# Five of six modulation groups summed on VectorE instead of TensorE

## The chip, the cores and the metric

The kernel runs on one core of one Trainium2 chip. The core has five engines with a queue of instructions each: TensorE (matrix products), VectorE, ScalarE, GpSimd and SyncE, which issues most DMAs. The metric is the device time of one execution in microseconds (us), as the median of three runs.

## The reference, cut to what matters

The reference has two blocks, a two-layer latent transformer and a block that ends in a mixture of experts, on 256 tokens of 1024 features. What the change touches is the modulation of the first block: two vectors (one for the latents, one for the context) times a 1024 x 6144 matrix per layer.

```python
silu_c = jax.nn.silu(c)
silu_cc = jax.nn.silu(c_ctx)
for layer in range(DEPTH):
    mod = (silu_c @ w_mod[layer] + b_mod[layer])[:, None, :]
    mod_c = silu_cc @ w_mod[layer] + b_mod[layer]
    shift1, scale1, gate1, shift2, scale2, gate2 = jnp.split(mod, N_MOD, axis=-1)
    c_shift1, c_scale1, c_gate1, c_shift2, c_scale2, c_gate2 = jnp.split(mod_c, N_MOD, axis=-1)
    ...
    h = modulate(rms_norm(x, norm_mix[layer]), shift1, scale1)
    ...
    x = x + gate1 * x_mix
    x = x + gate2 * swiglu(modulate(rms_norm(x, norm_ffn[layer]), shift2, scale2),
                           w_gate_up[layer], w_down[layer])
```

In the last layer the context stream is only used for its keys and values, so only c_shift1 and c_scale1 of that layer are needed.

## The kernel before, in words

Activations lie feature by feature: 128 features on the partitions, tokens along the free axis, eight chunks for the 1024 features. Layer 0 handles latents and context together (512 columns), layer 1 only the latents (256 columns, apart from the keys and values of the context). Every weight unit and every activation is split in two float32r parts, and a product is three matmuls (`mm3`). The first part is written by ScalarE, the second (source minus first part) by VectorE; `divide` does both.

The program is a set of Python generators, and a planner writes out the order of the instructions at build time. Class `Timer` (line 213) estimates when each engine is through; `stall` (511) says how long TensorE would wait for something; `drive` (525) steps the first generator whose inputs are there; `fill` (553) makes a step of a queue of side work when nothing else is ready, and `background` (566) makes one after each weight unit of a `gemm` (623). `tick` (473) emits deferred VectorE work whose inputs are there, and the weight loads and splits. `finish` (587) drives a queue to its end at once. All engine calls go through one wrapper, so that nearly every instruction has line 288; tiles tell them apart.

The modulation of one layer comes in three groups of 16 feature chunks, and each group has 16 tiles of w_mod: [128 rows of chunk k, 1024 columns], 512 KB. `modulation` (798) runs over the eight k and two halves. For each tile it makes two matmuls on quarters of the array: the 32 columns of `cs` (the two activated vectors, the rest zeros) times 512 columns of w_mod, summed in one PSUM tile over k. Then ScalarE copies the sums, TensorE turns them, and VectorE adds the bias into `mod`. In the trace these matmuls read `u,cs`; each float32 matmul has two records, so a chunk has four.

Group 0 of layer 0 runs at the start, where the first norm needs it. The other groups are entries of `self.bg`: groups 1 and 2 of layer 0 from line 1410 on, to be finished before the output projection (1447); group 0 of layer 1 during layer 0's feed-forward part (1472); groups 1 and 2 of layer 1 during layer 1 (1410). So a chunk stands where `background` or `fill` put it, and the rest where `finish` forces it. w_mod is loaded two tiles ahead (1411), ten ahead for one stretch (1451).

All big tiles share a pool of 42 buffers `u` of 4 KB per partition. SyncE issues the loads in order, and a load waits until the earlier users of its buffer are through. The second block ends with the experts, whose weights are streamed through the same buffers (`pump`, 1944).

Of the kernel before, what the change touches and what calls it, by code (L numbers as in the profile page):

```python
# [2 lines left out]

# [7 lines left out]
F32 = mybir.dt.float32  # L11
# [22 lines left out]
# ---------------------------------------------------------------- host layout  # L34
# [6 lines left out]
def _units(w):  # L41
    """[K, N] -> [N/128, 128 rows, K/128, 128 columns]"""
    k, n = w.shape
    return np.ascontiguousarray(w.reshape(k // 128, 128, n // 128, 128).transpose(2, 1, 0, 3))


def column_parameters(p):
    """Every per-feature vector as columns of one [128, n] array, and where each one starts."""
# [32 lines left out]
def shape_tables():  # L81
    t = {}
    # axial rotary embedding of the first block, feature-major; the sign of the pair swap is in the sine
# [8 lines left out]
    # discrete Fourier transform on odd frequencies  # L92
# [7 lines left out]
    # filter positions and decay  # L100
# [10 lines left out]
    # rotary embedding of the second block: inverse frequency and sign of the swapped half, per partition  # L111
# [4 lines left out]
    # 8 * log of how many of the dilated branches let query i see key j  # L116
# [6 lines left out]
    # before[t', t] = t' < t; descending weights that break ties; slot numbers  # L123
# [45 lines left out]
# ---------------------------------------------------------------- order of the program  # L169

class Null:
    """Stands for every object of the program in the pass that only finds the order of the weight tiles."""
# [22 lines left out]
class Part:  # L195
    """The two float32r parts of a tile.  ready: the n pieces of the program that fill it are there; eta: when they
    are expected to have run."""
# [15 lines left out]
class Timer:  # L213
    """Estimates when each engine will be through with its instructions, and when each tile will be there."""
# [48 lines left out]
    def there(self, x):  # L263
        if isinstance(x, float):
            return x
        if isinstance(x, Part):
            if x.ready:
                return self.there(x.ap)
            return FAR if x.eta is None else x.eta
        if not isinstance(x, bass.AP):  # L270
            return 0.0
        return self.wrote.get(x.name, (0.0, ""))[0] + self.LAG


class Engine:
    """An engine whose instructions are also given to the timer."""
# [26 lines left out]
class Stream:  # L303
    """The weight tiles that one chain of generators uses, in their order.  Loads run ahead; a unit (128 columns) is
    split ahead into two float32r parts."""
# [20 lines left out]
    def prepare(self):  # L326
        """split the next unit"""
# [8 lines left out]
    def run(self):  # L336
        """loads and splits ahead"""
# [13 lines left out]
    def get(self, *key, unit=True):  # L351
        """the next tile: a generator, which ends with the tile, or with the two parts of a unit"""
# [23 lines left out]
class Squares:  # L376
    """Sums of the squares of x for each token.  x comes in four pairs of chunks, each [128, 2, T] cut as gemm cuts
    its output; the first three are added up before they are summed over the partitions"""
# [39 lines left out]
class Net:  # L418
    TOL = 0.15
    EASE = 1.5  # L420
    PACE = 1.5
# [10 lines left out]
    def __init__(self, tc, a, at, orders, dbg, stop):  # L432
# [5 lines left out]
        self.fillers, self.bg = [], []  # L438
# [8 lines left out]
    # ---- allocation  # L447
# [16 lines left out]
    def ahead_of(self, n):  # L464
        """split n weight units ahead"""
        self.W.loads, self.W.splits = n + self.MORE, n

    # ---- order of the instructions
    def defer(self, fn, *deps, engine="DVE"):
        """fn emits instructions of an engine once deps are expected to be there when the engine comes to them"""  # L470
        self.pending.append((deps, engine, fn))

    def tick(self):
        """deferred instructions whose inputs are there; loads and splits of weights"""
# [11 lines left out]
        for s in self.streams:  # L486
            s.run()
        while len(self.piece) < self.ahead and t.free["DMA"] < t.free["PE"] + 2:
# [8 lines left out]
    def force(self):  # L497
        """the deferred instructions whose inputs are there first"""
# [12 lines left out]
    def stall(self, deps):  # L511
        """how long the tensor engine would wait"""
# [3 lines left out]
    def step(entry):  # L516
        """one step of [generator, what the step reads]; False if it can do nothing yet, None at its end"""
# [7 lines left out]
    def drive(self, *gens, extra=()):  # L525
        """all of the generators to their ends: the first of those whose inputs are there makes a step.  A generator
        yields what its next step reads, or BLOCK.  extra: entries that come second, but need not end"""
# [25 lines left out]
    def fill(self, *queues):  # L553
        """a step of the first entry of a queue, if its inputs are there"""
# [11 lines left out]
    def background(self):  # L566
        """a step of the work that only has to be done some time later"""
# [3 lines left out]
    def wait(self, *deps):  # L571
        """steps of the fillers while the tensor engine would wait"""
# [5 lines left out]
    def run(self, gen):  # L578
        """a generator to its end, with the fillers in its gaps"""
# [7 lines left out]
    def finish(self, queue):  # L587
        while queue:
            self.tick()
            if self.step(queue[0]) is None:  # L590
                queue.pop(0)

    # ---- pieces
    def divide(self, items, parts=(), then=None):
        """hi = float32r(src), lo = src - hi for each (hi, lo, src) or (hi, lo, src, factor of src); then the
        parts are ready"""
# [26 lines left out]
    def gemm(self, keys, xs, T=512, n=None, cuts=None, together=False, stream=None):  # L623
        """unit . xs for each weight unit, as a list of PSUM tiles [128 features, n units, T]; a generator.  xs may
        still grow to n; with cuts xs is a list of lists, and the k range between two cuts has its own output;
        together: the units side by side, each chunk of xs used as soon as it is there"""
# [50 lines left out]
    def pair(name, *idx, tail=()):  # L677
        """the two units of a pair of chunks: the last index counts pairs"""
# [3 lines left out]
    def by_tile(t, T):  # L682
        """[128, 2 chunks, T] cut as gemm cuts its output"""
# [5 lines left out]
    def pairs(self, T):  # L689
        """an endless row of tiles [128, 2, T]"""  # L690
# [5 lines left out]
    def chunks(self, n, T, pieces=1):  # L696
        """n places for the two float32r parts of [128, T]; and the parts of each two as gemm cuts its output"""
# [18 lines left out]
    def token_sums(self, ps, accs, first=True, last=True):  # L716
        """ps[128 tokens, tile] = sum over the partitions (and over accs) of acc[:, tokens]"""
# [6 lines left out]
    def rsqrt(self, ps, n, mul, add):  # L724
        """(ps*mul + add) ** -0.5"""
# [6 lines left out]
    def spread(self, ps, r):  # L732
        """ps[:, token] = r[token] in every partition"""
# [3 lines left out]
    def rms(self, accs, width, eps=1e-6):  # L737
        """PSUM tile with the reciprocal root mean square of each token in every partition"""
# [5 lines left out]
    def spread_rms(self, ps, width, eps=1e-6):  # L744
        """the same from the sums of the squares"""
# [7 lines left out]
    def modulated(self, xs, rb, gain, shift, out, streams=(0, 1), early=False):  # L753
        """parts of x*rb*gain + shift for pairs x[128, 2, T]; gain, shift: functions (chunk, stream) -> column;
        early: all the x*rb in a first step"""
# [28 lines left out]
    def norm_gain(self, xs, rb, name, out):  # L784
        """parts of x*rb*gain for x in pairs [128, 2, 256]"""
# [11 lines left out]
    # ---- modulation  # L797
    def modulation(self, l, grp):
        """columns grp*16 .. grp*16+15 (of 128 features) of both modulation vectors"""
# [29 lines left out]

    def gain_columns(self, l, which, m):  # L830
        """norm gain * (1 + scale)"""
        g = self.cp.tile([128, KC, 2], F32, name=f"g{which}{l}")
        for s in range(2):
# [4 lines left out]
    # ---- hyena filter and its spectrum  # L838
    def sin_of(self, ps, i):
        """sin(freq*(ps + b)) for [128, 256]"""  # L840
# [8 lines left out]
    def reduce_angle(self, r, a, n):  # L849
        """r = a - 2*pi*round(a / 2*pi), within [-pi, pi]"""  # L850
# [15 lines left out]
    def dft_tables(self, which, use, shape, **axes):  # L866
        """the two parts of a table; a generator"""
# [14 lines left out]
    def spectra(self, z, w1, w23):  # L882
        """spectra of the hyena filters of both layers; the layers' hidden units are in the two halves"""
# [44 lines left out]
    # ---- first block: one layer  # L928
# [1432 lines left out]
```

## Time and profile before

| | |
|---|---|
| median of 3 runs | 2087.15 us (2084.54 to 2092.17) |
| profiled execution, its span | 2082.8 us |
| instructions | 28349 |
| TensorE matmuls busy | 1986.3 us (95%) |
| TensorE weight loads busy | 1450.8 us (70%) |
| VectorE busy | 945.7 us (45%) |
| ScalarE busy | 718.3 us (34%) |
| HBM read | 428.13 MB, 207 GB/s over the span |

The profiled execution is known by its span, from the first to the last instruction; what lies around it is in the times of the runs alone, whose median is 4.35 us longer. A timeline row gives the start, the length, the engine, the line, the operation with the tiles it writes and reads, and how many instructions were merged; in square brackets the idle time before it and what ended it. Busy time of TensorE counts pipelined matmuls whose ends are modelled.

### The profile page before, as it was taken

The numbers are of one execution on the slowest core, as the hardware profiler recorded it, in microseconds if no ns is written. First come the engines' busy times: TensorE is split into PE (matmuls) and PEld (weight loads), VectorE is DVE, ScalarE is ACT, GpSimd is POOL, SyncE is SP. The second block draws the span as 40 slices with busy tenths as digits, with TensorE's granted clock in tenths as the row PEclk, the third lists the DMA queues.
The fourth block names the chain that finished last, engine by engine and source line by source line (L and its number), as shares of the span: only waits on it lengthen the run. The fifth ranks groups of instructions, "written<-read, shape, count | busy, mean of one in ns | idle before, by whom it ended". The sixth has DMA issues, their size and how long they took to land. (4 is left out here: it accounts for less than half of the span.)

```text
span 2082.8 us, 28349 instructions
## 1 busy us (share of the span) xinstructions
PE 1986.3 (95%) x11415; PEld 1450.8 (70%) x11415; DVE 945.7 (45%) x1624; ACT 718.3 (34%) x1171; POOL 39.8 (2%) x49
## 2 busy tenths in 40 slices
PE   7999999999999999999999999999999898888886
PEld 3777877776778888889888999998799541111111
DVE  6665755145334333576764755568654310000001
ACT  3433665224222322363653543444734110000001
POOL 0000000000000000000000000000010000000000
PEclk9999999999999999999999999999999999999999
DMA  9423224464223233444357455553257999999997
GB/s 366 132 81 101 62 82 150 164 236 174 96 88 114 89 91 100 134 170 149 114 188 245 164 189 172 178 183 94 100 167 295 377 419 420 419 419 419 419 420 318
DMA packets 121438, 432.13 MB, mean 207 GB/s; under 512 B 13654, under 2 KB 14152, under 8 KB 121304
## 3 DMA queue, kind: packets, MB, share of 16 engines
q1 hardware_dynamic: 119464, 424.64, 55.7%
q0 software_dynamic: 1696, 5.38, 0.8%
q8 instruction: 91, 1.49, 0.3%
q14 instruction: 43, 0.35, 0.0%
q10 hardware_dynamic: 144, 0.26, 0.0%
HBM read 428.13 MB, written 2.10 MB: 207 GB/s over the span
## 5 line engine op out<-in xcount | busy, mean ns | idle before, releaser
L288 PE MATMUL ps<-u 128*128 128x256 f32 (+2 forms) x9088 | 1599.8, 345 | 28.1 <-DMA u<-w 15.9
L288 PEld LDWEIGHTS ps<-u 128*128 128x128 f32 (+1 forms) x9088 | 1289.0, 186 | 348.1 <-DMA u<-w 101.3
L288 DVE TENSOR_TENSOR u<-u 128x1024 fp32r<-128x1024 f32 (+4 forms) x414 | 433.1, 1071 | 269.6 <-ACT u L288 226.2
L288 ACT ACTIVATE u<-u 128x1024 fp32r<-128x1024 f32 (+3 forms) x392 | 360.3, 960 | 286.9 <-DVE u L288 237.0
L288 PE MATMUL ps<-u,t 128*32 128x512 f32 (+1 forms) x1028 | 214.9, 610 | 30.8 <-DMA u<-w 18.2
L288 PEld LDWEIGHTS ps<-u,t 128*32 128x32 f32 (+1 forms) x1028 | 44.2, 110 | 185.8 <-DMA u<-w 114.5
L288 ACT ACTIVATE u<-ps 128x512 f32<-128x512 f32 (+3 forms) x207 | 91.7, 488 | 237.0 <-PE ps L288 236.3
L288 DVE TENSOR_TENSOR t<-t,ps 128x512 f32<-128x512 f32 x12 | 8.3, 688 | 258.9 <-PE ps L288 258.9
L288 ACT ACTIVATE t<-ps 128x512 f32<-128x512 f32 x57 | 33.4, 595 | 252.5 <-PE ps L288 252.4
L288 DVE TENSOR_TENSOR u<-u,ps 128x512 f32<-128x512 f32 x53 | 36.4, 687 | 128.4 <-PE ps L288 128.3
L288 PE MATMUL ps<-u,cs 128*32 128x512 f32 x384 | 86.1, 644 | 0.0
L288 DVE TENSOR_TENSOR u<-ps,u 128x128 fp32r<-128x128 f32 (+2 forms) x135 | 59.6, 491 | 48.9 <-ACT u L288 42.7
L288 DVE SCALAR_TENSOR_TENSOR u<-ps,mod,u 128x256 f32<-128x256 f32 x96 | 41.7, 479 | 79.9 <-PE ps L288 79.6
L288 ACT ACTIVATE u<-t 128x512 fp32r<-128x512 f32 (+1 forms) x74 | 41.8, 592 | 102.9 <-DVE t L288 91.7
L288 ACT ACTIVATE u<-ps,s 128x512 fp32r<-128x512 f32 (+1 forms) x26 | 15.8, 640 | 149.0 <-PE ps L288 145.8
L288 DVE SCALAR_TENSOR_TENSOR u<-ps,s,u 128x512 fp32r<-128x512 f32 (+2 forms) x24 | 15.4, 662 | 113.2 <-ACT u L288 90.9
L288 ACT ACTIVATE t<-ps,s 128x256 f32<-128x256 f32 (+1 forms) x80 | 49.1, 620 | 41.2 <-DVE s L288 40.2
L288 POOL TENSOR_TENSOR s<-s,mhalf 128x4 f32<-128x4 f32 (+2 forms) x25 | 28.5, 1141 | 1608.4 <-DVE s L288 1527.1
L288 PE MATMUL ps<-ident,t 128*128 128x128 f32 x332 | 46.8, 275 | 9.5 <-DVE t L288 7.0
L288 ACT ACTIVATE t<-u 128x512 f32<-128x512 f32 x41 | 25.2, 627 | 85.3 <-DVE u L288 85.2
L288 PEld LDWEIGHTS ps<-ident,t 128*128 128x128 f32 x332 | 37.8, 141 | 23.6 <-DVE t L288 14.3
L288 DVE TENSOR_REDUCE s<-ps 128x1 f32<-128x512 f32 (+2 forms) x65 | 38.9, 621 | 33.2 <-PE ps L288 32.9
(126 smaller groups left out, 682.6 us busy)
## 6 DMA issues: line engine op xcount, KB each, us to landing
u<-w SPq DMA_DIRECT2D x381, 512.0 KB, 9.9
u<-w_in SPq DMA_DIRECT2D x102, 512.0 KB, 3.9
u<-w_mod SPq DMA_DIRECT2D x96, 512.0 KB, 5.0
u<-w_gu SPq DMA_DIRECT2D x88, 512.0 KB, 3.7
u<-w_dn SPq DMA_DIRECT2D x32, 512.0 KB, 3.5
u<-w_out SPq DMA_DIRECT2D x24, 512.0 KB, 4.5
u<-w_oa SPq DMA_DIRECT2D x16, 512.0 KB, 4.0
u<-w_dn SPq DMA_DIRECT2D x16, 384.0 KB, 3.1
```

The costliest lines, as they stand in the source:

```text
L288: return fn(*args, **kw)
```

## The change

A new generator, `modulation_sums`, takes the place of `modulation` for five of the six groups. For each half of a group it keeps one accumulator [128, 1024] in a `u` buffer for each vector that is needed: both vectors for the groups 1 and 2 of layer 0 and group 0 of layer 1, only the latents' for groups 1 and 2 of layer 1. VectorE multiplies the tile of chunk 0 by the column of `cs` (TENSOR_SCALAR), and adds each further chunk with one SCALAR_TENSOR_TENSOR (tile times column plus accumulator). That makes 16 accumulators, 16 + 112 operations. Then TensorE sums the partitions: 32 columns of ones times 512 columns of an accumulator, two matmuls for each vector on quarters of the array, ten times in all. Copy, four transposes and bias follow as before, for half a group at a time.

The generators sit in a queue of their own, `self.sums`, which `tick` steps whenever the planner believes that TensorE would not wait for the step; each vector operation yields VectorE's estimated end less 0.3 us, and the tolerance is 0.15. w_mod is loaded three tiles ahead throughout. `finish(self.sums)` stands where `finish(self.bg)` does. `rotary_tables` and `memory_norm` stay in `self.bg`. The rest of the diff removes comments.

```diff
+    BEHIND = 0.3
...
     def tick(self):
...
         for s in self.streams:
             s.run()
+        while self.sums and not self.dry and self.stall(self.sums[0][1]) <= self.TOL:
+            if self.step(self.sums[0]) is None:
+                self.sums.pop(0)
...
+    def modulation_sums(self, l, grp):
+        nc = self.nc
+        vectors = (0, 1) if (l, grp) in ((0, 1), (0, 2), (1, 0)) else (0,)
+        for half in range(2):
+            acc = [self.u([128, 1024]) for _ in vectors]
+            for k in range(KC):
+                w = yield from self.W_mod.get("w_mod", l, grp, k, half, unit=False)
+                for s, a in zip(vectors, acc):
+                    c = self.cs[:, k, s:s + 1]
+                    if k == 0:
+                        nc.vector.tensor_scalar(a, w, c, None, op0=OP.mult)
+                    else:
+                        nc.vector.scalar_tensor_tensor(a, w, c, a, op0=OP.mult, op1=OP.add)
+                    yield (lambda: self.timer.free["DVE"] - self.BEHIND,)
+                del w
+            yield acc
+            ps = self.ps()
+            for i, (s, b) in enumerate((s, b) for s in vectors for b in range(2)):
+                nc.tensor.matmul(ps[32 * i:32 * i + 32, :], self.ones32, acc[s][:, b * 512:(b + 1) * 512],
+                                 start=True, stop=True, tile_position=(0, 32 * i))
+            del acc, a
+            n = 64 * len(vectors)
+            t = self.tmp()
+            nc.scalar.activation(t[:n], ps[:n], AF.Copy)
+            yield (t,)
+            pt = self.ps()
+            for b in range(4):
+                nc.tensor.transpose(pt[:, b * n:(b + 1) * n], t[:n, b * 128:(b + 1) * 128], self.ident[:n, :n])
...
+            for s in vectors:
+                nc.vector.tensor_add(m[:, :, :, s], src[:, s, :, :, 0], bias)
+            yield
...
-                self.W_mod.loads = 2
...
-        self.bg = self.before[l, 1]
-        self.W_mod.loads = 2
+        self.bg, self.sums = self.before[l, 1], self.sums_before[l, 1]
+        self.W_mod.loads = 3
...
         self.finish(self.bg)
+        self.finish(self.sums)
...
-        if l == 0:
-            self.W_mod.loads = 10
...
-            self.before = {(0, 1): entry(*m0), (0, 2): entry(m1[0], self.rotary_tables(), self.memory_norm()),
-                           (1, 1): entry(*m1[1:]), (1, 2): []}
+            self.sums_before = {(0, 1): entry(*m0), (0, 2): entry(m1[0]), (1, 1): entry(*m1[1:]), (1, 2): []}
+            self.before = {(0, 1): [], (0, 2): entry(self.rotary_tables(), self.memory_norm()), (1, 1): [], (1, 2): []}
```

How the order moves, at two places. First TensorE, from the end of layer 0's mix to its feed-forward part, before. `u` are weights and activations, `u,cs` the modulation, `ones` and `ident,s` the statistics of the norm between the output projection and the feed-forward part:

```order
L288 MATMUL ps<-u 128x512 x48
L288 MATMUL ps<-u,cs 32x512 x10
L288 MATMUL ps<-ident,t 128x128 x4
L288 MATMUL ps<-u 128x512 x168
L288 MATMUL ps<-ones,acc 128x1 x4
L288 MATMUL ps<-u 128x512 x24
L288 MATMUL ps<-ones,t 128x1 x8
L288 MATMUL ps<-ident,s 128x128 x4
L288 MATMUL ps<-u,cs 32x512 x20
L288 MATMUL ps<-u 128x512 x72
L288 MATMUL ps<-u,cs 32x512 x2
```

The same place now, from the last sum of layer 0's groups, which stands early in the mix, to the first sum of layer 1's group 0:

```order
L289 MATMUL ps<-u,ones_87 32x512 x4
L289 MATMUL ps<-u 128x512 x12
L289 MATMUL ps<-ident,t 128x128 x4
L289 MATMUL ps<-u 128x512 x552
L289 MATMUL ps<-ones_87,acc 128x1 x4
L289 MATMUL ps<-u 128x512 x24
L289 MATMUL ps<-ones_87,t 128x1 x8
L289 MATMUL ps<-ident,s 128x128 x4
L289 MATMUL ps<-u 128x512 x204
L289 MATMUL ps<-u,ones_87 32x512 x4
```

The ten forced matmuls and their transposes before the output projection are gone, and nothing stands between the statistics and the feed-forward part.

Second VectorE, in layer 0's first projections, where the short convolutions read PSUM (`ps,cols`) and weights are split (`u<-u 128x1024`), before:

```order
L288 TENSOR_TENSOR u<-u 128x1024 x3
L288 SCALAR_TENSOR_TENSOR t<-ps,cols,t 128x2x255 x4
L288 TENSOR_TENSOR u<-u,t 128x512 x2
L288 TENSOR_TENSOR u<-u 128x1024 x2
L288 SCALAR_TENSOR_TENSOR u<-ps,cols,u 128x2x255 x4
```

The same place now:

```order
L289 TENSOR_TENSOR u<-u 128x1024 x3
L289 SCALAR_TENSOR_TENSOR u<-u,cs 128x1024 x6
L289 SCALAR_TENSOR_TENSOR t<-ps,cols,t 128x2x255 x4
L289 TENSOR_TENSOR u<-u,t 128x512 x2
L289 TENSOR_TENSOR u<-u 128x1024 x2
L289 SCALAR_TENSOR_TENSOR u<-u,cs 128x1024 x4
L289 SCALAR_TENSOR_TENSOR u<-ps,cols,u 128x2x255 x4
```

Ten new operations (`u<-u,cs`) have come between the old ones, whose order is kept.

## Rows read from the trace of the kernel before

**Rows 1.** Page, part 1: engine, busy us, share of the span, instructions.

```profile
PE 1986.3 (95%) x11415; PEld 1450.8 (70%) x11415; DVE 945.7 (45%) x1624; ACT 718.3 (34%) x1171; POOL 39.8 (2%) x49
```

**Rows 2.** Table of stretches: us, busy time of each engine, clock, DMA share, GB/s.

```profile
51.00:357.00 306.00, 304.28 (x1485) 240.16 (x1484) 189.26 (x402) 151.31 (x286) 8.57 (x6) 0.99 0.30 97
518.00:690.00 172.00, 171.80 (x756) 136.72 (x757) 72.08 (x106) 50.57 (x67) 2.64 (x3) 1.00 0.32 105
882.00:1145.00 263.00, 260.95 (x1912) 227.78 (x1911) 170.62 (x301) 135.17 (x225) 8.29 (x7) 1.00 0.51 173
1640.00:2083.00 443.00, 379.04 (x1720) 96.72 (x1714) 35.80 (x59) 27.14 (x49) 1.29 (x2) 0.99 1.00 407
```

**Rows 3.** TensorE's timeline around one modulation chunk in layer 0's mix.

```profile
393.82 1.05 PE L288 MATMUL ps<-u,cs 128*32 128x512 f32 x4
394.80 11.18 PE L288 MATMUL ps<-u 128*128 128x512 f32 x48
```

**Rows 4.** Page, part 5: the modulation's matmuls; busy us, mean ns, idle before.

```profile
L288 PE MATMUL ps<-u,cs 128*32 128x512 f32 x384 | 86.1, 644 | 0.0
```

**Rows 5.** TensorE's timeline at the end of layer 0's mix.

```profile
454.28 2.77 PE L288 MATMUL ps<-u,cs 128*32 128x512 f32 x20
457.75 0.66 PE L288 MATMUL ps<-ident,t 128*128 128x128 f32 x4 [0.70 <-ACT t L288]
458.16 2.10 PE L288 MATMUL ps<-u 128*128 128x512 f32 x8
```

**Rows 6.** TensorE's timeline at layer 1's start and at its mix's end.

```profile
895.11 2.77 PE L288 MATMUL ps<-u,cs 128*32 128x512 f32 x20
897.81 2.42 PE L288 MATMUL ps<-u 128*128 128x256 f32 x18
...
1145.52 1.06 PE L288 MATMUL ps<-u,cs 128*32 128x512 f32 x8
...
1148.71 3.47 PE L288 MATMUL ps<-u 128*128 128x256 f32 x27
```

**Rows 7.** VectorE's timeline: second parts of the normed input, layers 1 and 0.

```profile
896.55 2.49 DVE L288 TENSOR_TENSOR u<-t,u 128x512 fp32r<-128x512 f32 x4
...
517.46 4.90 DVE L288 TENSOR_TENSOR u<-t,u 128x512 fp32r<-128x512 f32 x8
```

**Rows 8.** TensorE's timeline between layer 0's statistics and its feed-forward part.

```profile
508.93 1.11 PE L288 MATMUL ps<-ident,s 128*128 128x128 f32 x4 [1.38 <-POOL s L288]
509.97 6.79 PE L288 MATMUL ps<-u,cs 128*32 128x512 f32 x40
...
518.20 2.10 PE L288 MATMUL ps<-u 128*128 128x512 f32 x8 [1.00 <-DVE u L288]
```

**Rows 9.** Table of stretches, TensorE alone: us, busy, granted clock, DMA share, GB/s.

```profile
508.00:509.00 1.00, 0.07 (x1) 0.50 1.06 434
...
514.00:515.00 1.00, 1.00 (x12) 0.68 0.76 266
515.00:516.00 1.00, 1.00 (x16) 1.00 1.05 426
```

**Rows 10.** VectorE's instructions by shape: count, busy us, mean ns, idle before.

```profile
L288 DVE TENSOR_TENSOR u<-u 128x1024 fp32r<-128x1024 f32 x301 | 359.4, 1221 | 238.8 <-ACT u L288 197.5 <-issue 23.0 <-PE ps L288 17.5
L288 DVE TENSOR_TENSOR u<-u 128x512 fp32r<-128x512 f32 x71 | 48.2, 689 | 20.3 <-ACT u L288 19.1
...
L288 DVE SCALAR_TENSOR_TENSOR t<-u,cols,t 128x256 f32<-128x256 f32 x60 | 25.0, 478 | 0.0
...
L288 DVE TENSOR_SCALAR t<-t,s 128x512 f32<-128x512 f32 x19 | 9.2, 487 | 0.7
```

**Rows 11.** Waits of TensorE, 51 to 1160 us: total us, times, longest.

```profile
PE ps L288 <- DVE u L288: 4.7, 4, 1.6
```

**Rows 12.** Instructions on w_mod: time from issue to landing of its loads.

```profile
DMA to landing us min/median/max: 3.4/5.0/10.7
```

More of the change, by code (lines that the diff above doesn't have):

```diff
@@ L2 @@
 import itertools
+import types
 import numpy as np
@@ L270, in there @@
         if not isinstance(x, bass.AP):
-            return 0.0
+            return x() if isinstance(x, types.FunctionType) else 0.0
         return self.wrote.get(x.name, (0.0, ""))[0] + self.LAG
@@ L437, in __init__ @@
         self.pending = collections.deque()
-        self.fillers, self.bg = [], []
+        self.fillers, self.bg, self.sums = [], [], []
         self.ahead, self.piece, self.todo = 0, collections.deque(), self.pieces()
@@ L589, in finish @@
             self.tick()
-            if self.step(queue[0]) is None:
+            if queue and self.step(queue[0]) is None:
                 queue.pop(0)
@@ L828, in modulation @@
         yield
+    def modulation_sums(self, l, grp):
[26 more added lines that the diff above has]
+                nc.tensor.transpose(pt[:, b * n:(b + 1) * n], t[:n, b * 128:(b + 1) * 128], self.ident[:n, :n])
+            src = pt[:, :4 * n].rearrange("p (b v i s) -> p v i b s", b=4, v=len(vectors), i=2)
+            m = self.mod[l][:, grp * 16 + half * 8:grp * 16 + half * 8 + 8, :].rearrange("p (i b) s -> p i b s", b=4)
+            bias = self.col(f"b_mod{l}", grp * 16 + half * 8, 8).rearrange("p (i b) -> p i b", b=4)
+            for s in vectors:
+                nc.vector.tensor_add(m[:, :, :, s], src[:, s, :, :, 0], bias)
+            yield
     def gain_columns(self, l, which, m):
         g = self.cp.tile([128, KC, 2], F32, name=f"g{which}{l}")
-        for s in range(2):
+        for s in range(1 if (l, which) == (1, "ffn") else 2):
             self.nc.vector.scalar_tensor_tensor(g[:, :, s], self.mod[l][:, m * 8:m * 8 + 8, s], 1.0,
@@ L1447, in layer @@
         self.finish(self.bg)
+        self.finish(self.sums)
         gate1 = lambda j, s: mod[:, 16 + j, s:s + 1]
         sums = Squares(self, T)
-        if l == 0:
-            self.W_mod.loads = 10
         if l:
@@ L1471, in layer @@
             pass
-        self.bg = self.before[l, 2]
+        self.bg, self.sums = self.before[l, 2], self.sums_before[l, 2]
         self.drive(self.ffn(l, h, T, then))
@@ L2310, in program @@
             self.rope_t = cp.tile([128, 2, SEQ], F32, name="rope_t")
-            self.ones = cp.tile([128, 1], F32, name="ones")
-            nc.vector.memset(self.ones, 1.0)
+            self.ones32 = cp.tile([128, 32], F32, name="ones32")
+            nc.vector.memset(self.ones32, 1.0)
+            self.ones = self.ones32[:, 0:1]
             self.mhalf = cp.tile([128, 8], F32, name="mhalf")
@@ L2323, in program @@
             entry = lambda *gens: [[g, ()] for g in gens]
-            m0, m1 = ([self.modulation(l, g) for g in range(l == 0, 3)] for l in range(2))
+            m0, m1 = ([self.modulation_sums(l, g) for g in range(l == 0, 3)] for l in range(2))
             self.start_second()
-            self.before = {(0, 1): entry(*m0), (0, 2): entry(m1[0], self.rotary_tables(), self.memory_norm()),
-                           (1, 1): entry(*m1[1:]), (1, 2): []}
+            self.sums_before = {(0, 1): entry(*m0), (0, 2): entry(m1[0]), (1, 1): entry(*m1[1:]), (1, 2): []}
+            self.before = {(0, 1): [], (0, 2): entry(self.rotary_tables(), self.memory_norm()), (1, 1): [], (1, 2): []}
             self.layer(0, sums[0], self.squares(sums[1], 512), entry(spectra))
```

## The prediction

> **What bounds the kernel now.** I read the busy times first: TensorE 1986.3 of 2082.8 us, VectorE 945.7 [rows 1]. So TensorE is the suspect, and the next question is whether it is so at the place that changes. The table of stretches answers it [rows 2]: in the stretches of the first block that hold the moved work (51 to 357, 518 to 690, 882 to 1145 us) TensorE is busy 304.3 of 306, 171.8 of 172 and 261.0 of 263 us, and VectorE 189.3, 72.1 and 170.6 us. The last stretch, 1640 to 2083, has another bound: the DMA share is 1.00 at 407 GB/s.
>
> [...] A row on the moved matmuls themselves settles it here: a plain matmul after such a step starts 0.98 us after the step did (393.82 to 394.80), with no idle time named [rows 3]. That is time on the path, and the sum below goes by it.
>
> **What is removed.** All 96 chunks of w_mod cost TensorE 86.1 us, in 384 records, four to a chunk [rows 4]. 16 chunks are group 0 of layer 0, which stays. The other 80 stand in the timeline as 58 steps alone among other matmuls, and four runs of 5, 10, 5 and 2 steps.
> - 58 alone, 0.98 us each [rows 3]: 56.8 us.
> - Run of 5 at the end of layer 0's mix, forced there: 454.28 to 458.16 with the wait for ScalarE and the transposes, 3.9 us [rows 5]. The next matmuls need the last merged chunk, which is made in this time too; I take 3.0.
> - Run of 2 at the end of layer 1's mix: 1145.52 to 1148.71, 3.2 us [rows 6]; I take half, 1.6, for the same reason.
> - Run of 5 at 895.11 to 897.81 [rows 6]: it fills the wait for the normed input, whose second parts VectorE makes from 896.55 on [rows 7]. I take 0.6 of 2.7.
> - Run of 10 at 509.97 [rows 8]: it fills the wait for layer 0's second norm. VectorE makes the second parts from 517.46 on [rows 7], and TensorE waits for them until 518.20 even with the filler. Worth 0.
> - Transposes of the three other groups, 0.4 us each (457.75 to 458.16) [rows 5]: 1.1.
>
> Removed: 56.8 + 3.0 + 1.6 + 0.6 + 1.1 = 63.1 us.
>
> **What is added to TensorE.** Ten sums over the partitions. Six have four matmuls of 32 columns; eight records in a run took 1.06 us [rows 6], taken as 1.0. Four have two, 0.98 us [rows 3]. Together 9.9. Four transposes each, 0.4 us [rows 5], 3.8. Their copies on ScalarE have other matmuls behind them in the new order, so nothing for these; if the cover is gone, each is worth the 0.70 us of the old wait [rows 5].
>
> [...]
>
> **What is added to VectorE.** Sixteen accumulators: 16 TENSOR_SCALAR and 112 SCALAR_TENSOR_TENSOR of 128x1024. No row has this shape. One with two SBUF operands took 478 ns at 256 columns, and a TENSOR_TENSOR goes from 689 ns at 512 to 1221 at 1024, so 1.04 ns a column [rows 10]: 0.478 + 768 x 0.00104 = 1.28 us alone. Bounds are 1.22 (the TENSOR_TENSOR itself) and 1.91 (four times 478). I take 1.22, nearest to the row of the same length, since neighbours overlap a little. TENSOR_SCALAR took 487 ns at 512; between that and twice it, 0.75. Sum: 112 x 1.22 + 16 x 0.75 = 149 us.
>
> It goes 74, 37 and 37 us to the three stretches (64, 32 and 32 operations). The stretches become shorter by what TensorE saves: about 293, 169 and 241 us. VectorE would be busy 263 of 293 (90%), 109 of 169 (64%) and 208 of 241 (86%). It fits, but tightly, and the planner fills whatever gap it believes in, up to 0.45 us beyond TensorE's own time. Queued behind such an operation are second parts of weights (two units ahead, so harmless), second parts of activations, softmax sums, and the four or two matmuls that wait for an accumulator. TensorE now waits for VectorE 4.7 us in four waits over 51 to 1160 us [rows 11]. One operation in front of an urgent one costs up to 1.22 us. Bounds: 0, if every one falls into a real gap, and 137 us, if all 112 come in the way. I take 12 us, ten late ones of 1.22: one for each of the ten sums, where the new order makes TensorE wait for the accumulator itself. That is nearer to zero because the row nearest to it is the 4.7 us.
>
> Loads: the 80 transfers stay, three ahead in place of two (ten at one place). They land in 5.0 us median, 10.7 at most [rows 12], and now VectorE waits for them in order. Priced at nothing while three ahead cover it; else it is part of the first rival.
>
> **Sum.** 63.1 - 9.9 - 3.8 - 2.9 - 12 = 34.5 us. The profiled execution's span is 2082.8 us, so 2048.3; the median of the runs is 4.35 us above that span, so 2087.15 - 34.5 = 2052.7, say 2053. The saving lies before the last stretch, whose DMAs set the end; it carries over because the experts' loads wait for buffers that earlier work frees, and the order of the second block is the same in both programs.
>
> **Rivals.**
> - VectorE gives the saving back. Its place is 51 to 357 us, where it would be 90% busy. The saving without lateness is 46.5 us; at 1.22 us each it is gone when 38 of the 112 operations stand before something urgent, or when loads that land at 10.7 in place of 5.0 us hold VectorE about eight times. For it: the gaps there are small. Against: 64% and 86% elsewhere. Gives 2067 to 2098.
> - The same decides for slower. At 47 operations in the way (57 us) the time is 2098, at 56 (68 us) it is 2109. This needs VectorE to be the bound in attention, where most of its work is softmax that TensorE waits for.
> - Half rate. The scalar-tensor-tensor at half rate takes the time of 1024 more columns, 1.22 + 1.07 = 2.3 us. Then VectorE needs 324 of 293 us in the first stretch: 31 us late there and some 15 more in layer 1, so 34.5 - 46 = -12, 2099. The row of 478 ns at 256 columns against it: half rate would add 256 columns at 1.04 ns and make 0.74. [...]
> - More than forecast: no lateness at all, and the covered runs worth half: 2030 to 2041.
> - The change does not do what it says, since the DMA-bound end begins when it began: 2087. Against it stands that its loads follow the buffers.
>
> **How the numbers follow.** Forecast (2041 to 2066): 0.58. More: 0.10. VectorE gives it back, still faster: 0.06; within 0.5%: 0.13. Slower by lateness: 0.06. Half rate: 0.03. Hidden at the end: 0.04. A change of 0.5% (10.4 us) is about what a measurement of this kernel can tell from none. Faster 0.74, same 0.17, slower 0.09. The range 2035 to 2088 leaves out the better half of "more", the slower cases and the last third of "within 0.5%", 0.18 together.
>
> **What would show it.** The step after a unit gone, 48 plain matmuls following 48 without a hole; TensorE standing still before 518 with the clock at 0.50 behind it; the new operation at 1.2 to 1.3 us; VectorE about 1095 us busy; TensorE's waits for VectorE near 17 us in the first block. Waits of over 45 us there, or an operation of over 2 us, would prove me wrong.

## The result, and the profile after

The changed kernel takes 2062.64 us (median of 4 runs, 2062.21 to 2065.21) against 2088.4 us of the kernel before (4 runs, 2084.54 to 2092.17). The ratio is 0.987, 95% interval 0.9856 to 0.9884: faster by 25.8 us. The time is within the range given, and 10 us above the forecast of 2053. The profiled execution took 2062.49 us, with a span of 2060.7.

Part 1 of its page (engine, busy us, share of the span, instructions), against [rows 1]:

```profile
PE 1935.8 (94%) x11179; PEld 1449.0 (70%) x11179; DVE 1085.6 (53%) x1759; ACT 715.9 (35%) x1170; POOL 41.2 (2%) x49
```

Two groups of VectorE's instructions by shape (count, busy us, mean ns, idle before), against [rows 10]:

```profile
L289 DVE SCALAR_TENSOR_TENSOR u<-u,cs 128x1024 f32<-128x1024 f32 x112 | 140.1, 1278 | 0.8 <-DMA u<-w_mod 0.7
...
L289 DVE TENSOR_SCALAR u<-u,cs 128x1024 f32<-128x1024 f32 x16 | 12.0, 748 | 5.0 <-PE ps L289 5.0
```

The new operation takes 1.28 us, and the wait for a tile of w_mod costs VectorE 0.7 us in all. So neither the half rate nor late loads are at work.

The table of stretches after the change (us, busy time of TensorE, weight loads, VectorE, ScalarE and GpSimd, clock, DMA share, GB/s) answers to [rows 2]: the first projections and attention, the feed-forward part, layer 1, and the experts, last of all:

```profile
51.00:332.00 281.00, 271.74 (x1366) 224.42 (x1364) 244.63 (x453) 142.04 (x272) 9.92 (x6) 0.99 0.36 115
...
497.00:665.00 168.00, 166.41 (x735) 135.03 (x736) 107.25 (x139) 51.48 (x67) 2.68 (x3) 0.99 0.43 135
...
850.00:1110.00 260.00, 248.69 (x1838) 234.41 (x1837) 210.50 (x342) 138.68 (x232) 8.40 (x7) 0.98 0.53 179
...
1610.00:1970.00 360.00, 311.46 (x1422) 80.49 (x1424) 27.81 (x45) 19.65 (x33) 0.58 (x1) 0.99 1.03 409
```

TensorE now stands idle 9.3 us in the first (1.7 before) and 11.3 us in the third (2.1 before). The last line holds the surprise: the DMAs are as busy as before, and move 409 GB/s. In the same part of the kernel before it was more, by the same view:

```profile
1640.00:2000.00 360.00, 316.27 (x1474) 83.17 (x1469) 27.82 (x45) 20.03 (x34) 0.58 (x1) 0.99 1.03 419
```

Where the time went is read from instructions that both programs have. The timeline of TensorE gives their starts in us: the sums of squares ahead of layer 0's second norm (A), at layer 1's start (B) and ahead of its second norm (C); the first matmuls of the second block that wait 0.36 us for VectorE (D); the end of the experts' first group (E, a wait of 0.35 us); the last eight matmuls (F).

| | A | B | C | D | E | F | E to F |
|---|---|---|---|---|---|---|---|
| before | 498.32 | 882.02 | 1172.20 | 1360.91 | 1662.65 | 2071.68 | 409.0 |
| changed | 477.01 | 861.02 | 1139.43 | 1327.12 | 1628.87 | 2049.47 | 420.6 |
| ahead by | 21.3 | 21.0 | 32.8 | 33.8 | 33.8 | 22.2 | |

Two rows of each kernel's timeline (start, length, engine, line, operation, count, idle before), D and F, before:

```profile
1360.91 5.18 PE L288 MATMUL ps<-u 128*128 128x256 f32 x41 [0.36 <-DVE u L288]
...
2071.68 2.60 PE L288 MATMUL ps<-u 128*128 128x512 f32 x8
```

and after:

```profile
1327.12 5.18 PE L289 MATMUL ps<-u 128*128 128x256 f32 x41 [0.36 <-DVE u L289]
...
2049.47 2.59 PE L289 MATMUL ps<-u 128*128 128x512 f32 x8
```

At D the change has brought 33.8 us, of 34.5 forecast. The experts then give 11.6 back. Two questions follow: why the expert stretch became longer, and whether the 33.8 are made up as the prediction said.

### The profile page after: what moved, and what is told of

The parts are those of the page before. It is cut to its first block, busy times and chain, and to the rows that moved or that the text cites. A ratio compares the mean times of both kernels' runs of the same rounds, so it can differ in the third digit from the quotient of the medians.

```text
span 2060.7 us, 28054 instructions
## 1 busy us (share of the span) xinstructions
PE 1935.8 (94%) x11179; PEld 1449.0 (70%) x11179; DVE 1085.6 (53%) x1759; ACT 715.9 (35%) x1170; POOL 41.2 (2%) x49
## 5 line engine op out<-in xcount | busy, mean ns | idle before, releaser
L289 DVE SCALAR_TENSOR_TENSOR u<-u,cs 128x1024 f32<-128x1024 f32 x112 | 140.1, 1278 | 0.8 <-DMA u<-w_mod 0.7
L289 ACT ACTIVATE t<-ps 128x512 f32<-128x512 f32 (+1 forms) x62 | 36.2, 594 | 266.3 <-PE ps L289 266.2
L289 DVE TENSOR_TENSOR u<-ps,u 128x128 fp32r<-128x128 f32 (+2 forms) x135 | 59.9, 490 | 29.2 <-ACT u L289 22.9
L289 PE MATMUL ps<-ident,t 128*128 128x128 f32 (+1 forms) x352 | 49.0, 273 | 7.4 <-DVE t L289 7.3
L289 PEld LDWEIGHTS ps<-ident,t 128*128 128x128 f32 (+1 forms) x352 | 39.7, 140 | 19.4 <-DVE t L289 14.9
```

The lines of the kernel that those rows point to most:

```text
L289: return fn(*args, **kw)
```

## Experiments

A median carries some 4 us of the execution's own: the kernel before had a median of 2086.2 in ten runs and of 2090.1 in thirteen on the same chip, and the profile of its repetition lost 4.5 us between 1611 and 1667 us, at a clock of 0.83 in four stretches of 10 us. Where that matters, landmarks decide.

**The rate: chip or kernel?** Both kernels again, unchanged.

> The kernel before, unchanged, on the same chip as the next three. The profiles so far leave one thing open: the changed kernel is 33.8 us ahead at the start of the expert stretch and 22.2 us ahead at its end, with 409 GB/s there against 419 GB/s before. Theory A: the rate belongs to the chip or the execution, not to the kernel. Then this run and the next show the same rate (within 1 GB/s), and the lead that the changed kernel has at the start of the stretch stands at its end; 2087 us if the rate is 419, some 2096 if it is 409. Theory B: the rate belongs to the kernel (to the order in which its buffers are used). Then this run shows 419 GB/s and 2087 us, the next one 409.

> The changed kernel, unchanged, on the same chip as the run before it. Theory A (rate of the chip): the same rate as that run; 2053 us at 419 GB/s, 2063 at 409, some 34 us below that run's kernel either way. Theory B (rate of the kernel): 409 GB/s and 2063 us whatever the other run shows, 25 us below it.

Measured: 2086.21 us (10 runs) and 2064.65 us (4 runs, ratio to the kernel before 0.9891, 0.9871 to 0.9911). The table of stretches without engines (us, clock, DMA share, GB/s), of the kernel before, repeated:

```profile
1700.00:1900.00 200.00, 1.00 1.03 419
```

and of the changed kernel, repeated:

```profile
1700.00:1900.00 200.00, 1.00 1.03 409
```

The rate belongs to the kernel (theory B). The order of SyncE's loads and of TensorE's work is the same in both second blocks (SyncE's last 502 loads are those of the kernel before, one by one). What differs is where the buffers lie. The change makes the tile of ones 32 columns wide, 128 B in place of 32 B per partition, and that tile stands ahead of the 42 big buffers. As the build places them, their first one starts at byte 51968 of the partition before (203 x 256) and at 52064 after, 96 B past a multiple of 256. All 42 lie 4096 B apart, so all are off it. These addresses are those of the build; no trace shows them. The runs show what each shift of the buffers does.

**The start of the buffers, alone.** Four kernels.

```diff
 # before_shift96: the kernel before, tile of ones as long as after the change
-            self.ones = cp.tile([128, 1], F32, name="ones")
+            self.ones = cp.tile([128, 32], F32, name="ones")[:, 0:1]
 # the changed kernel: n = 72 (after_aligned), 64 (after_shift224), 40 (after_shift128)
-            self.ones32 = cp.tile([128, 32], F32, name="ones32")
+            self.ones32 = cp.tile([128, n], F32, name="ones32")[:, 0:32]
```

> The kernel before with one edit: its tile of ones has 32 columns in place of 1 (only the first is used), as in the changed kernel. That makes the tile 128 B instead of 32 B long, and every tile behind it, the 42 big buffers among them, starts 96 B later in each partition; instructions and their order stay. The two profiles of each kernel showed 419 GB/s for the kernel before and 409 for the changed one in the expert stretch, on the same chip. Theory: the start of the buffers sets the rate (51968 B, a multiple of 256, against 52064). Then this kernel shows 409 GB/s there, and it is 9 to 11 us slower than the kernel before (some 175 MB move at the lower rate: 418 us become 428), about 2098. Rival: the rate comes from the order in which the buffers are used; then it shows 419 GB/s and the time of the kernel before. [...]

> The changed kernel with one edit: the tile of 32 ones is allocated with 72 columns, so that the big buffers start at 52224 B, a multiple of 256, in place of 52064. Nothing else moves. Theory (the start of the buffers sets the rate): 419 GB/s in the expert stretch, where the changed kernel shows 409; the lead that it has at the start of that stretch (33.8 us) stands at its end, and the kernel is 9 to 11 us faster than the changed kernel, about 2053, which is what was predicted. Rival (order of use): 409 GB/s and the time of the changed kernel, 2063.

> The changed kernel with the tile of ones at 64 columns: the big buffers start 224 B past a multiple of 256 in place of 96 B. Theory one: the distance from the boundary counts, so the rate falls below the 409 GB/s of 96 B. Theory two: any start off the boundary costs the same, so 409 GB/s and 2063 us as in the changed kernel. [...]

> The changed kernel with the tile of ones at 40 columns: the big buffers start 128 B past a multiple of 256. 96 and 224 B past it both gave 409 GB/s in the expert stretch, a multiple of 256 gave 419. Theory: any start off a multiple of 256 costs the same, so 409 GB/s. Rival: what counts is a smaller boundary (128, 64 or 32 B would all be met by this start, and 64 B is missed by both 96 and 224), so 419 GB/s.

| | start past a multiple of 256 B | GB/s, 1700 to 1900 us | E to F, us | median, us |
|---|---|---|---|---|
| before, repeated | 0 | 419 | 410.6 | 2086.21 |
| before_shift96 | 96 | 409 | 421.1 | 2097.45 |
| changed, repeated | 96 | 409 | 420.5 | 2064.65 |
| after_aligned | 0 | 420 | 409.4 | 2051.20 |
| after_shift224 | 224 | 409 | 420.7 | 2064.08 |
| after_shift128 | 128 | 409 | 420.7 | 2060.98 (one run) |

The row of the first, the kernel before with nothing but its tile of ones lengthened:

```profile
1700.00:1900.00 200.00, 0.99 1.03 409
```

and of the second, the changed kernel with the tile lengthened once more, to a multiple of 256:

```profile
1700.00:1900.00 200.00, 1.00 1.03 420
```

The start of the buffers switches the rate on and off in both kernels, and with it 11 us of the expert stretch. before_shift96 is slower than the kernel before (ratio 1.0037, 1.0021 to 1.0052, where 9 to 11 us were expected and the medians show 6.6; E to F shows 10.5). after_aligned takes 2051.20 us (4 runs, 2051.0 to 2056.63; ratio 0.981, 0.9788 to 0.9832); its profile is of the slowest of the four. The distance from the boundary does not count: 96, 128 and 224 B all give 409. So theory two of after_shift224 held, and 128 B is no boundary that helps.

**VectorE's part, taken out.** The accumulating operation is left out, so seven chunks of eight are missing from the sums. The `continue` skips the planner's pause behind the operation as well, and the tile of w_mod is free at once. So the run prices the operation together with the buffers that it holds and the order that it causes.

```diff
-                        nc.vector.scalar_tensor_tensor(a, w, c, a, op0=OP.mult, op1=OP.add)
+                        continue
```

> The changed kernel without the 112 accumulating operations on VectorE: of each sum only the first chunk counts, so seven chunks of eight are left out of the modulation; loads, sums over the partitions, copies and transposes all stay. It prices VectorE's part alone. By the prediction the saving without lateness is 46.5 us: TensorE's waits for VectorE between 51 and 1160 us fall from 23.6 to about 10 us (the 4.8 us after layer 0's second norm stay), the lead at the start of the expert stretch is 46 us, and the time is 12 us below the changed kernel, about 2051. Rival: the DMA-bound end takes the gain, the lead at its start is 46 us and the time stays within 3 us of the changed kernel.

Measured: 2050.55 us (4 runs), 14.1 below the changed kernel on the same chip; A to E at 463.94, 844.77, 1125.27, 1312.96 and 1614.72. At D it is 48.0 us ahead of the kernel before, where the sum without lateness was 46.5. So VectorE's operations cost 48.0 - 33.8 = 14.2 us, where 12 were put (16.4 against the changed kernel's repetition, whose D is at 1329.34); the expert stretch passed the gain on. But the waits did not fall to 10 us. TensorE's waits for VectorE, 51 to 1160 us (total, times, longest), of this kernel:

```profile
PE ps L289 <- DVE u L289: 18.1, 11, 4.8
```

and of the changed kernel, against [rows 11]:

```profile
PE ps L289 <- DVE u L289: 23.6, 14, 4.8
```

Most of these waits are there without one accumulation. By stretches the gain is 34.4 us up to A, 2.9 from A to B, 9.7 from B to C (changed kernel: 21.3, -0.3, 11.8). VectorE's lateness is the difference: 13.1 us up to A, where it is 87% busy from 51 to 332 us, 3.2 from A to B, and none in layer 1, where the run without accumulation is 2.1 us the slower. The 13.1 are from one profile of either kernel; the profiles of the changed kernel, shifted or not, reach A between 476.9 and 482.7. Of the 13.1, TensorE's idle time from 51 us to A makes 8.1 (9.3 us with the accumulations, 1.2 without). An instance in VectorE's timeline of the changed kernel: an accumulation stands in front of the second part of an activation (`u<-ps,u`), for which TensorE waits 2.94 us, to 257.22. The accumulation is at most 1.2 us of that wait:

```profile
255.28 1.28 DVE L289 SCALAR_TENSOR_TENSOR u<-u,cs 128x1024 f32<-128x1024 f32 x1
256.48 1.28 DVE L289 TENSOR_TENSOR u<-ps,u 128x512 fp32r<-128x512 f32 x2
```

In layer 1 the waits are of another kind, as the next run suggests.

**Layer 1's sums earlier.**

```diff
-            self.sums_before = {(0, 1): entry(*m0), (0, 2): entry(m1[0]), (1, 1): entry(*m1[1:]), (1, 2): []}
+            self.sums_before = {(0, 1): entry(*m0), (0, 2): entry(*m1), (1, 1): [], (1, 2): []}
```

> The changed kernel with one move: groups 1 and 2 of layer 1 are queued behind group 0, so that VectorE sums them during layer 0's feed-forward part (where it was 37% busy from 665 to 850 us) in place of layer 1's attention (81% busy, 11.2 us of TensorE's waits for VectorE and a mean clock of 0.98). Theory: the 32 operations are late only where VectorE is nearly full. Then layer 1's waits for VectorE fall to about 2 us, its clock to 1.00 (up from 0.98), and the kernel is 9 to 13 us faster than the changed one, about 2051. Rival: lateness is a matter of the planner putting the operation in front of something urgent wherever it stands; then the waits move to 665 to 850 us and the time stays within 4 us.

Measured: 2059.72 us (4 runs, 2055.73 to 2062.69; ratio 0.9869, 0.9849 to 0.9889), 4.9 below the changed kernel of the same set, less than expected. Landmarks A to E: 478.45, 869.32, 1127.82, 1318.69, 1621.99. From A to B it takes 6.9 us longer than the changed kernel: four sums, at 1.7 us each, and no lateness from 32 more operations on VectorE. From B to C it takes 258.5 us against 278.4. The clock of layer 1 is back at 1.00; the waits are 7.0 us, not 2. One of them, TensorE's timeline of this kernel:

```profile
1008.09 4.22 PE L289 MATMUL ps<-u 128*128 128x256 f32 x22 [2.34 <-DVE u L289]
```

the same matmuls in the changed kernel:

```profile
1005.02 5.80 PE L289 MATMUL ps<-u 128*128 128x256 f32 x22 [2.35 <-DVE u L289]
```

and in the kernel before, where a chunk stands in front of them:

```profile
1003.94 1.05 PE L288 MATMUL ps<-u,cs 128*32 128x512 f32 x4
...
1006.58 2.90 PE L288 MATMUL ps<-u 128*128 128x256 f32 x22 [1.16 <-DVE u L288]
```

With or without accumulations in layer 1 the wait is 2.3 us; the chunk on TensorE had covered 1.2 us of it. (VectorE needs the same 5.0 us in all three from the sums that end its wait to the part that TensorE waits for.) That is cover that the change took away, not lateness. What this run gained, it lost in part behind C: 11.6 us ahead of the changed kernel at C, 8.4 at D, 6.9 at E.

**Operations held back.** VectorE's steps wait until VectorE is believed to be ahead; aligned buffers.

```diff
-    BEHIND = 0.3
+    BEHIND = -0.4
-        self.W_mod.loads = 3
+        self.W_mod.loads = 2
```

> The changed kernel with its big buffers at a multiple of 256 B and two numbers changed: a vector step now waits until VectorE is expected to be 0.25 us ahead of TensorE (BEHIND -0.4 in place of 0.3), and w_mod is loaded two ahead in place of three, without which there are too few buffers. Leaving the accumulation out gave 13.1 us in the stretch from 51 us to layer 0's second norm (the norm's sums at 463.9 against 477.0 us). Theory: that is lateness, operations put in front of something urgent. Then this kernel reaches the norm 5 to 8 us earlier than the changed kernel with aligned buffers and is that much faster than its 2051 us, about 2044. Rival: VectorE is simply full there (87%), so that operations held back come in the way later; then the norm is reached within 2 us of it and the time is 2049 to 2053.

Measured: 2084.65 us (10 runs; ratio 0.9987, 0.9973 to 1.0001), 33 us above after_aligned; the norm's sums at 484.08, against 482.68 in after_aligned. The rival was right about the norm, and its time, 2049 to 2053, was far too low. The sums that were held back are forced at the end of layer 1's mix, in TensorE's timeline:

```profile
1125.02 1.92 PE L289 MATMUL ps<-u,ones 128*32 128x512 f32 x4 [9.52 <-DVE u L289]
1127.62 0.69 PE L289 MATMUL ps<-ident,t 64*128 64x64 f32 x4 [0.68 <-ACT t L289]
1139.57 1.92 PE L289 MATMUL ps<-u,ones 128*32 128x512 f32 x4 [11.26 <-DVE u L289]
```

TensorE stands still for 20.8 of the 33 us in these two waits, and the granted clock is down between them (table of stretches, columns as above):

```profile
1130.00:1140.00 10.00, 0.43 (x2) 0.22 (x4) 9.21 (x8) 0.00 (x0) 0.00 (x0) 0.50 0.45 170
```

**The filler put back.** Group 0 of layer 1 on TensorE again; aligned buffers.

```diff
+                self.W_mod.loads = 2
...
+        if l == 0:
+            self.W_mod.loads = 10
...
-            self.sums_before = {(0, 1): entry(*m0), (0, 2): entry(m1[0]), (1, 1): entry(*m1[1:]), (1, 2): []}
-            self.before = {(0, 1): [], (0, 2): entry(self.rotary_tables(), self.memory_norm()), (1, 1): [], (1, 2): []}
+            self.sums_before = {(0, 1): entry(*m0), (0, 2): [], (1, 1): entry(*m1[1:]), (1, 2): []}
+            self.before = {(0, 1): [], (0, 2): entry(self.modulation(1, 0), self.rotary_tables(), self.memory_norm()), (1, 1): [], (1, 2): []}
```

> The changed kernel with aligned buffers and one part undone: group 0 of layer 1 is again made by TensorE alone, with its loads ten ahead, so that ten of its sixteen chunks stand in the wait for layer 0's second norm. The prediction put the run of ten at 0, and layer 0's feed-forward part gave nothing in the traces (21.3 us ahead at its start, 21.0 at its end). Theory: the filler there is free, and moving the other six chunks just pays for the two sums; the time is that of the changed kernel with aligned buffers, 2049 to 2052, with TensorE at a clock of 1.00 within 7 us of the filler's start. Rival: the moved group does earn its six chunks and its transposes, 6 us; then 2056 or more.

Measured: 2058.25 us (4 runs, 2058.07 to 2059.36), 7.0 above after_aligned; by the time alone the rival. The landmarks say otherwise for the part in question: from A to B it takes 383.7 us (476.81 to 860.55), after_aligned 383.8 and the kernel before 383.7. So this group's move is worth nothing, as predicted. The clock at the filler (us, TensorE busy, clock, DMA share, GB/s):

```profile
488.00:492.00 4.00, 4.00 (x23) 0.50 1.08 414
492.00:494.00 2.00, 2.00 (x16) 0.58 0.92 215
494.00:495.00 1.00, 1.00 (x16) 1.00 1.03 373
```

It is back at 1.00 within 6 us of the filler's start at 488.46. The 7 us arise later: layer 1 (B to C) takes 280.5 us against 278.2, and D to E 306.4 against 301.7, with a clock of 0.52 from 1450 to 1460 us, where after_aligned has 1.00. The four runs lie within 1.3 us of each other, but the landmarks are of one of them, and the unchanged kernel's repetition lost as much from D to E (305.9 us against 301.7). Why the clock falls there stays open.

**Combinations.** early_aligned is early with n = 72 columns.

> Both moves together: layer 1's groups 1 and 2 summed during layer 0's feed-forward part, and the big buffers at a multiple of 256 B. Theory: the two gains add, since the first lies before the expert stretch and the second in it: 419 GB/s there, some 5 us from the earlier sums and 10 from the rate below the changed kernel, about 2049. Rival: at the higher rate the expert stretch is bounded by the loads' buffers and not by the rate, so that only one of the two shows, 2053 or above.

Measured: 2050.38 us (4 runs, 2046.55 to 2053.32; ratio 0.980, 0.9775 to 0.9826), at 420 GB/s from 1700 to 1800 us: not to be told from after_aligned. At D it is at 1319.04, early's place, but from D to E it takes 308.9 us (after_aligned 301.7), with a clock of 0.55 from 1440 to 1450 us.

The other puts all together. The edit is shown against the kernel with the filler put back; `first_group` is that kernel's `modulation(1, 0)`, which sets `first_done` at its end:

```diff
-    BEHIND = 0.3
+    BEHIND = -0.4
...
+    def gated(self, *gens):
+        yield (lambda: 0.0 if self.first_done else FAR,)
+        for g in gens:
+            yield from g
...
-        self.W_mod.loads = 3
+        self.W_mod.loads = 2
...
-            self.sums_before = {(0, 1): entry(*m0), (0, 2): [], (1, 1): entry(*m1[1:]), (1, 2): []}
-            self.before = {(0, 1): [], (0, 2): entry(self.modulation(1, 0), self.rotary_tables(), self.memory_norm()), (1, 1): [], (1, 2): []}
+            self.sums_before = {(0, 1): entry(*m0), (0, 2): entry(self.gated(*m1[1:])), (1, 1): [], (1, 2): []}
+            self.before = {(0, 1): [], (0, 2): entry(self.first_group(), self.rotary_tables(), self.memory_norm()), (1, 1): [], (1, 2): []}
```

> All that looked good together: aligned buffers; group 0 of layer 1 on TensorE, filling the wait for the second norm; groups 1 and 2 of layer 1 summed by VectorE during layer 0's feed-forward part, behind that group; groups 1 and 2 of layer 0 summed as in the first run of this set (BEHIND -0.4, two loads ahead). Expected from the landmarks: 8 us from the earlier sums, 0 to 1 from the filler, 5 to 8 from the later steps, so 13 to 17 us below the changed kernel with aligned buffers, 2034 to 2038. Rival: the parts share one gain (VectorE's work in the way), and the expert stretch or the second block returns some of it; then 2043 to 2047.

Measured: 2056.74 us (4 runs, 2052.95 to 2060.07), above even the rival. The norm's sums come at 485.98, the feed-forward part takes 392.7 us; as in the run with held-back operations, A comes late. Which of the parts costs what was not separated. after_aligned and early_aligned are the fastest versions that leave nothing out, 11 to 14 us below the changed kernel.

## Why the prediction was right, and which step failed

- **The bound.** TensorE, in the first block: right. Taking work off it brought 33.8 us at D, although its weight loads were busy for only 70% of the span [rows 1].
- **The removal.** 46.5 us without lateness were forecast, and the run without accumulation shows 48.0. That they agree is luck, since two errors cancel. By the prediction's terms some 24 us lie ahead of A, 1 between A and B and 22 in layer 1; the run shows 34.4, 2.9 and 9.7.
- **Ahead of A: the price of a step.** The 0.98 us of [rows 3] run from the start of a step to the next plain matmul. The plain matmuls on either side of it are slower too. In the kernel before, the next step starts at 405.91, so the 48 plain matmuls of [rows 3] take 11.11 us:

```profile
405.91 1.05 PE L288 MATMUL ps<-u,cs 128*32 128x512 f32 x4
```

  The changed kernel makes 552 of the same shape without a break in 125.26 us, so 48 of them in 10.89:

```profile
351.75 125.42 PE L289 MATMUL ps<-u 128*128 128x512 f32 x552
477.01 0.94 PE L289 MATMUL ps<-ones,acc 128*128 128x1 f32 x8
```

  A step therefore cost 12.09 - 10.89 = 1.20 us and not 0.98, 6.0 us more for the 27 single steps ahead of A. TensorE's idle time from 51 us to A falls from 4.1 to 1.2 us, and the kernel before lost some 1.7 us there at a clock of 0.50 to 0.68 from 211 us on (an estimate from stretches of 2 us). With some 1.3 us off for four sums that were dearer than forecast this makes 33 of the 34.4; the last 1 us stays open.
- **Layer 1: the overlap.** The 25 single steps there were not all on the path, since chunks had stood in waits. TensorE alone (us, busy, clock, DMA share, GB/s), B to C, in the kernel before:

```profile
882.02:1172.20 290.18, 286.29 (x2119) 1.00 0.52 176
```

  and without accumulation:

```profile
844.77:1125.27 280.50, 265.69 (x2027) 0.99 0.54 183
```

  TensorE has 20.6 us less to do, but stands idle 14.8 us in place of 3.9. Its waits for VectorE rise from 2.1 to 12.7 us without a single accumulation.
- **The run of ten, worth 0.** Right: 21.3 us ahead at A, and again 21.3 behind the gap (518.20 before, 496.89 after, with 4.83 us of waiting in it). TensorE's timeline after, against [rows 8]:

```profile
487.62 1.12 PE L289 MATMUL ps<-ident,s 128*128 128x128 f32 x4 [1.37 <-POOL s L289]
491.26 0.80 PE L289 MATMUL ps<-u 128*128 128x512 f32 x1 [2.53 <-ACT u L289]
496.89 15.45 PE L289 MATMUL ps<-u 128*128 128x512 f32 x58 [4.83 <-DVE u L289]
```

- **The clock.** Predicted: 0.50 behind the gap; the sum has 2.9 us for it, a term that no run shows. The table of stretches, TensorE alone, against [rows 9]:

```profile
497.00:498.00 1.00, 1.00 (x3) 0.50 0.00 0
...
500.00:501.00 1.00, 1.00 (x4) 0.50 0.00 0
501.00:502.00 1.00, 1.00 (x6) 0.94 0.00 0
502.00:503.00 1.00, 1.00 (x6) 1.00 0.00 0
```

  TensorE was busy from 496.89 on, at 0.50 to 501 and at 0.94 in the next us. Half of these 4.1 us is 2.1 us lost, an estimate. The 58 matmuls from 496.89 took 15.45 us, where the pace of the 552 (125.42 us) makes 13.18: 2.3 us more, less than forecast. Not foreseen: the clock fell in layer 1 too, behind waits of 2 us (mean 0.98 from 850 to 1110 us; 0.66 from 1005 to 1010 us, behind a wait of 2.35 us).
- **TensorE's sums.** Forecast 0.98 and 0.38 us for four matmuls and four transposes of one vector; four such sums cost 1.7 us each from A to B in early. Here too the slower plain matmuls on either side were left out.
- **VectorE's operations.** 1.28 us, the value worked out for one alone, where 1.22 was taken; 0.75 for the others, as taken. Sum 152 us for 149. Half rate: refuted by 1278 ns beside 1220 ns of the plain two-operand form.
- **Lateness.** 12 us forecast, 14.2 measured, but not one for each sum: by these profiles 13.1 of it stand ahead of A, where the first rival put it. So the number is near, and its reason was not. The rival's mechanism is there; 38 late operations would have been needed for it to win. TensorE's waits for VectorE are 23.6 us over 51 to 1160 us, where 17 were named as a sign, but 18.1 of them stand without an accumulation.
- **What failed: "it carries over".** The loads do follow the buffers, and no lead was lost at the start of the stretch (33.8 us at D and at E). What was taken for granted in the same sentence is that the stretch itself lasts as long as before. Its term in the sum was 0 and should have been -11.6; with it the forecast is 22.9 us, and F shows 22.2. The reason was in the diff: a constant tile grew by 96 B, ahead of all 42 big buffers. With the buffers at a multiple of 256 B the kernel takes 2051.20 us, where 2053 was predicted.

## What to carry to other kernels

In a stretch that the DMAs bound, ask of a diff not only what it issues but where its tiles come to lie: a constant that grew by 96 B cost 11 us in a part of the program that the change doesn't touch. A saving on the busiest engine is best checked at landmarks that both programs share, stretch by stretch, since one total can be right by two errors. The price of a step that repeats is read from its whole period, beside the same work without it: the time to the next instruction gave 0.98 us where the period gives 1.20. Side work on a second engine is cheap where that engine has room (32 operations more in the feed-forward part, where VectorE had been 37% busy from 665 to 850 us, cost none, 64 in a stretch where VectorE came to 87% cost 13 us), and holding it back was no remedy: the deadline then forced it, 20.8 us of standing still.

## What the runs showed of the hardware

In the expert stretch, loads of 4096 B per partition ran at 419 to 420 GB/s where the target starts at a multiple of 256 B, and at 409 GB/s at 96, 128 and 224 B past one, at a DMA share of 1.03 each time. The loss did not grow with the distance. Why it does not is open.

The granted clock differed behind equal waits. Behind a wait of 2.35 us the changed kernel shows

```profile
1005.00:1010.00 5.00, 4.98 (x20) 0.66 0.00 0
```

and early, behind 2.34 us at the same matmuls,

```profile
1010.00:1015.00 5.00, 5.00 (x30) 1.00 0.53 168
```

(us, TensorE busy, clock, DMA share, GB/s). What decides it, these runs don't tell.
